# Second mixer, last 16 weight chunks: the low parts come from an accumulating transfer in place of VectorE

## The chip, the cores and the metric

The program runs on one core of a Trainium2 chip. Its engines are TensorE (PE in the profile; PEld is its weight load), VectorE (DVE), ScalarE (ACT), GpSimd (POOL) and SyncE (SP); the last two also issue the transfers of this kernel. The metric is the device time of one execution in microseconds (us), the median of several runs. Lower is better.

## The reference

Two transformer stacks follow each other on 256 tokens of width 1024, with 256 context tokens beside them in the first stack. The change lies in the first stack, whose second layer's mixer is cut to this:

```python
def _token_mixer(h, w_in, w_out, ...):
    z = h @ w_in
    u, v, q, f_fw, f_bw, i, og = jnp.split(z, cuts, axis=-1)
    a_out = _gmlp_spatial(u, v, w_s, b_s, g_v)
    o, s_f, s_b = _hgrn_bidir(q, f_fw, f_bw, i, lb_f, lb_b, s0_f, s0_b)
    o = _rmsnorm(o, g_o.reshape(HGRN_HEADS, HGRN_V)).reshape(B, L, B_W)
    b_out = o * jax.nn.silu(og)
    return jnp.concatenate([a_out, b_out], axis=-1) @ w_out, s_f, s_b
```

`_gmlp_spatial` multiplies gelu(u) by a mixed and normalised gelu(v). `_hgrn_bidir` is a gated linear scan over the tokens in both directions. All is float32; a matrix product with the weights is made here of three products of a faster type, in which each factor is split into a high and a low part.

## The kernel before, in words

Weights come from HBM in a fixed list of chunks (`plan`), mostly 128x1024 float32 (512 KB). For each chunk class `Weights` does three things. `load` (L171) issues the transfer into one of 4 buffers named `raw`, from SP. `hi_to` (L221) copies `raw` on ScalarE into `hi`, of the type that TensorE multiplies faster, which rounds it; there are 6 such buffers. `do` (L237) subtracts on VectorE, `lo` = `raw` - `hi`, into one of 5 buffers. A chunk's `raw` buffer is loaded anew once `lo` is made.

`mm3` multiplies: `hi` by the high part of the activations (L415), `hi` by their low part (L416), and `lo` by their high part (L417). A chunk of 128 columns and 256 tokens is 24 such matmuls.

The program is written in one order and every engine runs its own part of it in that order. `step` writes a chunk's matmuls, then what is to be done with the result of the chunk before (`flush`), then `ahead_hi`, which prepares later chunks, then `tick`, which advances the generators in `side`, then `ahead_lo`. `fits` says how far ahead a chunk may be prepared, by the ring of buffers.

The end of the second layer's mixer takes these chunks in this order: four of `og` (called OG0 to OG3 here), four of `u` (U0 to U3), and eight of `w_out` (WO0 to WO7). While OG and U run, the scan's second half (`hg`) advances by one level per chunk. One level is a product on TensorE (`scores`, L921), two products on VectorE (L997, L1000), a regrouping copy on ScalarE (`keys`, L928, output `Y`) that the next level's `scores` needs, and a masked copy (L1008; from the sixth level on copies on ScalarE, L1013). The spatial part (`gmlp`) runs beside it: squares on ScalarE (L1125), a power on GpSimd (L461), a scaling on ScalarE (L1132, output `vg`), and a product on TensorE (L1137).

WO0 to WO3 are then taken together: first each chunk's products with two of the eight inputs, chunk by chunk, and so on as inputs get ready, the last two of them made by L1085 from `yb`. WO4 to WO7 follow one by one. Behind WO7 come the sums of squares (L490), a broadcast (L504), and the next block's inputs (L523, L531).

Of the kernel before, what the change touches and what calls it, by code (L numbers as in the profile page):

```python
# [7 lines left out]
F32 = mybir.dt.float32  # L8
F32R = mybir.dt.float32r
U8 = mybir.dt.uint8  # L10
AF = mybir.ActivationFunctionType
ALU = mybir.AluOpType
# [97 lines left out]
class Pair:  # L110


    def __init__(self, hi, lo=None):
        self.t = [hi, lo]
# [2 lines left out]
        return self.t[i[1]][i[0], i[2]]  # L117


class Weights:  # L120


# [3 lines left out]
    def __init__(self, nc, flat, rawp, hlp, chunks, nraw, nhl):  # L126
        self.nc, self.flat, self.rawp, self.hlp = nc, flat, rawp, hlp
        self.sizes = [p[3] * p[5] for p in chunks]
        self.nraw, self.nhl = nraw, nhl
        self.offs = np.concatenate([[0], np.cumsum(np.array(self.sizes) * 128)]).tolist()  # L130
        self.units, self.ring, self.loads, self.work = [], [], [], []
        j = 0
        while j < len(chunks):
            p = chunks[j]
            u = len(self.units)
            if p[0].endswith("_w1") and (p[0][:4], p[1]) in FAST and p[4] // 128 >= FIRST_FAST:
                self.units += [(k, len(self.loads), j) for k in "axys"]
                self.work += [("s2", u), ("lo", u), ("lo", u + 1), ("s4", u), ("lo", u + 2), ("lo", u + 3)]
                self.loads.append(("p", j))
                j += 2  # L140
            else:
                self.units.append(("n", len(self.loads), j))
                self.work.append(("lo", u))
                self.loads.append(("n", j))
                j += 1
        r = 0
        for k, _, _ in self.units:
            self.ring.append(r)
            r += k != "s"
        self.n = len(self.units)  # L150
        self.n_load = self.n_hi = self.n_work = self.n_take = self.freed = 0
        self.n_pair = self.freed_pair = 0
        self.raw, self.hl, self.made, self.did = {}, {}, set(), {None}
        self.cur, self.held = 0, set()
        self.sp, self.room = None, 0
# [44 lines left out]
    def fits(self, u, part):  # L200

        if u >= self.n or self.units[u][1] >= self.n_load:
            return False
        if self.units[u][0] == "s":
            return sum(self.units[v][0] == "s" for v in self.made | self.held if v < u) < self.room
        return self.ring[u] <= self.ring[self.base] + self.nhl - 1 - (part == "lo")

    def ready(self, u):

# [3 lines left out]
    def hi_to(self, i):  # L213
        while self.n_hi <= min(i, self.n - 1):
            u = self.n_hi
            while not self.ready(u):
                self.do()
            self.dma_to(self.units[u][1])
            s = self.source(u)
            t = self.tile(u, "hi")  # L220
            self.nc.scalar.activation(out=t[:, :s.shape[-1]], in_=s, func=AF.Copy)  # L221
            self.hl[u] = Pair(t)
            self.made.add(u)
            self.n_hi += 1

    def do(self):

        k, u = self.work[self.n_work]
        _, l, j = self.units[u]
        self.dma_to(l)  # L230
        if k == "lo":
            self.hi_to(u)
            s = self.source(u)
            c = s.shape[-1]
            t = self.tile(u, "lo")
            w = self.hl[u]
            self.nc.vector.tensor_tensor(out=t[:, :c], in0=s, in1=w[:, 0, :c].bitcast(F32), op=ALU.subtract)  # L237
            w.t[1] = t
            if self.units[u][0] in "ns":
                self.raw.pop(l)  # L240
                self.freed += 1
                self.freed_pair += self.units[u][0] == "s"
        else:
            w, x = self.raw[l][:2]
            o, i = (x, w[:, 0:512]) if k == "s2" else (w, w[:, 512:1024])
            self.nc.vector.tensor_tensor(
                out=o[:, 512:1024], in0=(x[:, 0:512] if k == "s2" else x[:, 512:1024]), in1=i, op=ALU.add)
        self.did.add((k, u))
        self.n_work += 1
# [1917 lines left out]
```

## Time and profile before

| | before |
|---|---|
| median of 3 runs | 2401.54 us (2400.47 to 2401.78) |
| the profiled execution, its time | 2399.38 us |
| its span, first to last instruction | 2397.6 us |
| busy share of the span: PE, DVE, ACT, POOL | 99%, 69%, 44%, 4% |
| mean granted clock of TensorE | 0.999 |

In the rows of stretches stand the stretch and its length, then the busy time and the count of instructions of PE, PEld, DVE, ACT and POOL, the granted clock, the share of the transfer engines and GB/s. The times of the rows below count from the first instruction of the span. A busy share is a mean over stages that differ; the change lies between some 1490 us and 1580 us. The end of a matmul is modelled in this profile, so the distance between starts says more than its length.

### The profile page before, as it was taken

How to read it: one execution, taken by the hardware profiler on the slowest of the kernel's cores; microseconds unless marked ns; L12 is line 12 of the kernel's file. 1: busy time of each engine (PE TensorE's matmuls, PEld its weight loads, DVE VectorE, ACT ScalarE, POOL GpSimd, SP SyncE). 2: the span in 40 equal slices, each digit the busy share in tenths (PEclk: the TensorE clock that was granted, in tenths of full speed). 3: DMA queues.
4: the chain of work that ended last, by engine and by line, in shares of the span. 5: the costliest groups of instructions: out<-in, count | busy, mean ns of one | idle time of the engine just before them, and what ended most of it. 6: DMA issues, size and time to landing. Idle time of an engine off the chain costs nothing.

```text
span 2397.6 us, 39387 instructions
## 1 busy us (share of the span) xinstructions
PE 2368.5 (99%) x15852; PEld 2157.5 (90%) x15852; DVE 1652.1 (69%) x2670; ACT 1058.4 (44%) x1741; POOL 91.3 (4%) x136
## 2 busy tenths in 40 slices
PE   7999999999999999999999999999999999999999
PEld 5888888999888888898899999999999999999999
DVE  6788986637468888877575665765567677558653
ACT  4322223455342222244353454654466556446642
POOL 0000000000000000000101000000002000010000
PEclk9999999999999999999999999999999999999999
DMA  8555652222245556534555532355555465553663
GB/s 316 209 210 179 225 187 95 89 71 71 79 148 199 206 194 217 170 104 121 144 159 148 146 98 88 97 177 185 187 184 173 133 204 186 193 167 110 208 193 125
DMA packets 117447, 383.31 MB, mean 160 GB/s; under 512 B 12936, under 2 KB 19080, under 8 KB 117008
## 3 DMA queue, kind: packets, MB, share of 16 engines
q1 hardware_dynamic: 112368, 371.88, 46.0%
q0 software_dynamic: 4896, 8.92, 2.2%
q8 instruction: 124, 2.03, 0.3%
q14 instruction: 59, 0.48, 0.1%
HBM read 379.68 MB, written 1.06 MB: 159 GB/s over the span
## 4 chain that ended last, share of the span: by engine, by line
PE 91%; DVE 4%; issue 2%; ACT 2%; DMA 0%; POOL 0%; POOLq 0%; SPq 0%; DVEq 0%; ACTq 0%
PE mm L416 24%; PE mm L417 24%; PE mm L415 24%; PE mm L691 7%; PE mm L921 2%; PE mm L1459 2%; PE mm L1458 2%; PE mm L1460 2%; DVE lo L237 1%; PE mm L1115 1%; PE mm L1116 1%; PE mm L1117 1%; ACT hi L221 1%; PE aux L504 0%; PE mm L1555 0%
## 5 line engine op out<-in xcount | busy, mean ns | idle before, releaser
L221 ACT ACTIVATE hi<-raw 128x1024 fp32r<-128x1024 f32 (+2 forms) x544 | 554.3, 1029 | 425.0 <-PE mm L416 251.4
L415 PE MATMUL mm<-h,hi 128*128 128x256 f32 (+1 forms) x2188 | 726.2, 332 | 3.6 <-ACT h L531 2.4
L417 PE MATMUL mm<-h,lo 128*128 128x256 f32 (+1 forms) x2188 | 721.3, 330 | 0.4 <-DVE lo L237 0.2
L237 DVE TENSOR_TENSOR lo<-raw,hi 128x1024 fp32r<-128x1024 f32 (+2 forms) x544 | 642.7, 1188 | 105.2 <-PE mm L417 54.4
L416 PE MATMUL mm<-l,hi 128*128 128x256 f32 (+1 forms) x1804 | 614.3, 340 | 1.1 <-DVE l L1340 0.2
L415 PEld LDWEIGHTS mm<-h,hi 128*128 128x128 f32 x2188 | 413.1, 189 | 44.8 <-ACT h L531 2.6
L417 PEld LDWEIGHTS mm<-h,lo 128*128 128x128 f32 x2188 | 413.0, 189 | 42.9 <-DVE lo L237 1.2
L415 PE MATMUL mm<-g,hi 128*128 128x256 f32 (+1 forms) x1258 | 409.0, 325 | 0.0
L416 PE MATMUL mm<-g,hi 128*128 128x256 f32 (+1 forms) x1258 | 408.6, 325 | 0.0
L417 PE MATMUL mm<-g,lo 128*128 128x256 f32 (+1 forms) x1258 | 408.6, 325 | 0.0
L416 PEld LDWEIGHTS mm<-l,hi 128*128 128x128 f32 x1804 | 340.7, 189 | 43.9 <-DVE l L532 2.7
L399 DVE CUSTOM_DVE_ANT_0 jk<-ada,condb,vec 128x1024 f32<-128x1024 f32 x256 | 328.3, 1282 | 9.3 <-ACT condb L392 4.1
L417 PEld LDWEIGHTS mm<-g,lo 128*128 128x128 f32 x1258 | 236.6, 188 | 22.1
L415 PEld LDWEIGHTS mm<-g,hi 128*128 128x128 f32 x1258 | 236.7, 188 | 21.9
L416 PEld LDWEIGHTS mm<-g,hi 128*128 128x128 f32 x1258 | 236.7, 188 | 21.9
L538 DVE SCALAR_TENSOR_TENSOR xT<-mm,mods,xT 128x256 f32<-128x256 f32 x192 | 85.7, 479 | 119.3 <-PE mm L417 119.1
L767 ACT ACTIVATE g<-t 128x512 fp32r<-128x512 f32 (+1 forms) x71 | 40.2, 566 | 260.6 <-DVE t L765 260.6
L416 PE MATMUL mm<-h,hi 128*128 128x256 f32 x512 | 143.9, 281 | 0.0
L1458 PE MATMUL mm<-hi,h 128*128 128x256 f32 x384 | 111.1, 289 | 0.0
L1459 PE MATMUL mm<-lo,h 128*128 128x256 f32 x384 | 107.4, 280 | 0.1
L1460 PE MATMUL mm<-hi,h 128*128 128x256 f32 x384 | 107.3, 279 | 0.0
L765 DVE TENSOR_TENSOR t<-t,mm 128x512 f32<-128x512 f32 (+1 forms) x71 | 42.8, 603 | 78.6 <-PE mm L417 76.0
(329 smaller groups left out, 3294.3 us busy)
## 6 DMA issues: line engine op xcount, KB each, us to landing
raw<-wflat SPq DMA_DIRECT2D x463, 512.0 KB, 3.4
ada<-adaT SPq DMA_DIRECT2D x128, 512.0 KB, 4.2
raw<-wflat SPq DMA_DIRECT2D x64, 448.0 KB, 3.4
wy<-wflat SPq DMA_DIRECT2D x34, 256.0 KB, 4.5
ada<-ada SPq DMA_DIRECT2D x16, 512.0 KB, 10.0
wx<-wflat SPq DMA_DIRECT2D x17, 256.0 KB, 3.0
wx<-wflat POOLq DMA_DIRECT2D x17, 256.0 KB, 5.2
wy<-wflat POOLq DMA_DIRECT2D x17, 256.0 KB, 5.5
```

The lines of the kernel that those rows point to most:

```text
L221: self.nc.scalar.activation(out=t[:, :s.shape[-1]], in_=s, func=AF.Copy)
L237: self.nc.vector.tensor_tensor(out=t[:, :c], in0=s, in1=w[:, 0, :c].bitcast(F32), op=ALU.subtract)
L399: nc.vector.tensor_tensor_reduce(out=jk, in0=t, in1=condb[:, c, :], scale=1.0, scalar=V(f"bada{l}")[:, j:j + 1], op0=ALU.mult, op1=ALU.add ...
L415: nc.tensor.matmul(out, whi, xhi, start=start, stop=False)
L416: nc.tensor.matmul(out, whi, xlo, start=False, stop=False)
L417: nc.tensor.matmul(out, wlo, xhi, start=False, stop=stop)
L538: nc.vector.scalar_tensor_tensor(out=xT[:, o, t0:t1], in0=ps[:, t0:t1], scalar=gate(l, i, o, 0 if t0 == 0 else 1), in1=xT[:, o, t0:t1], op ...
L691: nc.tensor.matmul(ps[:, :256], a, b, start=start and k + m == 0, stop=k == 3 and m == 2, skip_group_check=not start)
L921: nc.tensor.matmul(sl(p, i), sl(Y, b + i), x(b + i), start=True, stop=True)
L1458: nc.tensor.matmul(p[:, :256], xhi, whi, start=(k == 0), stop=False)
L1459: nc.tensor.matmul(p[:, :256], xhi, wlo, start=False, stop=False)
L1460: nc.tensor.matmul(p[:, :256], xlo, whi, start=False, stop=(k == 7))
```

## The change

For 16 chunks (OG0 to OG3, U0 to U3 and WO0 to WO7 of the second layer) `lo` is no longer made by VectorE. `hi_to` makes both parts: ScalarE copies `raw` into `hi` as before, then writes the negated `hi` into `lo`, and GpSimd issues a transfer from `raw` to `lo` that adds, on the way, to what stands there. `do` then only frees the `raw` buffer in the count; the next load into that buffer waits for the adding transfer. Since `lo` must have a buffer at the time of `hi`, these chunks may be prepared 4 ahead and no longer 5.

```diff
+def lo_by_dma(p):
+
+    return p[1] == 1 and (p[0] == "w_out" or p[0] == "w_in" and p[4] in range(0, 512) or p[0] == "w_in" and p[4] >= 3072)
...
+        self.by_dma = {u for u, (k, _, j) in enumerate(self.units) if k == "n" and lo_by_dma(chunks[j])}
...
-        return self.ring[u] <= self.ring[self.base] + self.nhl - 1 - (part == "lo")
+        return self.ring[u] <= self.ring[self.base] + self.nhl - 1 - (part == "lo" or u in self.by_dma)
...
             t = self.tile(u, "hi")
             self.nc.scalar.activation(out=t[:, :s.shape[-1]], in_=s, func=AF.Copy)
             self.hl[u] = Pair(t)
+            if u in self.by_dma:
+                c = s.shape[-1]
+                lo = self.tile(u, "lo")
+                self.nc.scalar.activation(out=lo[:, :c], in_=t[:, :c].bitcast(F32), func=AF.Copy, scale=-1.0)
+                self.nc.gpsimd.dma_start(out=lo[:, :c].bitcast(F32), in_=s, accum_op=ALU.add)
+                self.hl[u].t[1] = lo
...
-            t = self.tile(u, "lo")
             w = self.hl[u]
-            self.nc.vector.tensor_tensor(out=t[:, :c], in0=s, in1=w[:, 0, :c].bitcast(F32), op=ALU.subtract)
-            w.t[1] = t
+            if u not in self.by_dma:
+                t = self.tile(u, "lo")
+                self.nc.vector.tensor_tensor(out=t[:, :c], in0=s, in1=w[:, 0, :c].bitcast(F32), op=ALU.subtract)
+                w.t[1] = t
```

The order of TensorE and of SP stays as it was, and VectorE's is the same without the 16 subtractions. ScalarE's changes at three places that the prediction speaks of. Rows of the changed kernel carry its own line numbers: L227 is the copy into `hi`, L232 the negation, L233 the adding transfer, and from L250 on each number is 13 above that of before (L941 there is L928 here).

The first place is ScalarE from the last product of `v` on. Before, from the two copies that start at 1500.29 us:

```order
L221 ACTIVATE hi<-raw 128x1024 x2
L936 COPY at<-mm 128x512
L928 COPY Y<-Wt_13112 128x512
L1125 ACTIVATE t,ss<-vg 128x128 x4
L1196 ACTIVATE vg<-mm 128x256
L1132 ACTIVATE vg<-vg,ss 128x128 x4
L1196 ACTIVATE vg<-mm 128x256
L221 ACTIVATE hi<-raw 128x1024 x2
L1125 ACTIVATE t,ss<-vg 128x128 x4
L1099 ACT_TABLE_LOAD
L1099 ACTIVATE yb<-mm 128x256
L221 ACTIVATE hi<-raw 128x1024
```

Of the change, the same stretch as far as the second pair:

```order
L227 ACTIVATE hi<-raw 128x1024
L232 ACTIVATE lo<-hi 128x1024
L227 ACTIVATE hi<-raw 128x1024
L232 ACTIVATE lo<-hi 128x1024
L949 COPY at<-mm 128x512
L941 COPY Y<-Wt_13113 128x512
L1138 ACTIVATE t,ss<-vg 128x128 x4
L1209 ACTIVATE vg<-mm 128x256
L1145 ACTIVATE vg<-vg,ss 128x128 x4
L1209 ACTIVATE vg<-mm 128x256
L227 ACTIVATE hi<-raw 128x1024
L232 ACTIVATE lo<-hi 128x1024
```

Each copy has its negation behind it, ahead of the work that stood there; the copies are those of a chunk one place earlier in the list than before.

The second place is ScalarE at the scan's last level, behind U2's result. Before, where the last row is the copy of WO4:

```order
L1085 ACTIVATE YE<-a_12357 128x256
L221 ACTIVATE hi<-raw 128x1024
L928 COPY Y<-Wt_13112 128x512
L1013 COPY at<-mm 32x4x32 x4
L1103 ACTIVATE t<-mm 128x256
L221 ACTIVATE hi<-raw 128x1024
```

Of the change, where the last two rows are the copy and the negation of WO3:

```order
L1098 ACTIVATE YE<-a_12357 128x256
L227 ACTIVATE hi<-raw 128x1024
L232 ACTIVATE lo<-hi 128x1024
L941 COPY Y<-Wt_13113 128x512
L1026 COPY at<-mm 32x4x32 x4
L1116 ACTIVATE t<-mm 128x256
L227 ACTIVATE hi<-raw 128x1024
L232 ACTIVATE lo<-hi 128x1024
```

WO3's high part has moved from ahead of the last `Y` to behind it, with the negation after it.

The third place is ScalarE behind the last two inputs of `w_out`. Before, where the copies are those of WO5 and WO6:

```order
L1085 ACTIVATE h_13800<-yb 128x256
L1085 ACTIVATE h_13804<-yb 128x256
L221 ACTIVATE hi<-raw 128x1024
L543 ACT_TABLE_LOAD
L543 ACTIVATE dummy<-epsc 128x1
L475 ACTIVATE acc<-xT 128x256
L221 ACTIVATE hi<-raw 128x1024
```

Of the change, where they are those of WO4 and WO5:

```order
L1098 ACTIVATE h_13810<-yb 128x256
L1098 ACTIVATE h_13814<-yb 128x256
L227 ACTIVATE hi<-raw 128x1024
L232 ACTIVATE lo<-hi 128x1024
L556 ACT_TABLE_LOAD
L556 ACTIVATE dummy<-epsc 128x1
L488 ACTIVATE acc<-xT 128x256
L227 ACTIVATE hi<-raw 128x1024
L232 ACTIVATE lo<-hi 128x1024
```

Here too each chunk is one place later than before, and has a negation more.

## Rows read from the trace of the kernel before

**Rows 1.** The page's span, and VectorE's subtraction from 1500 to 1560 us

```profile
span 2397.6 us, 39387 instructions
L237 DVE TENSOR_TENSOR lo<-raw,hi 128x1024 fp32r<-128x1024 f32 x12 | 14.5, 1217 | 1.6 <-ACT hi L221 1.6
```

**Rows 2.** Busy time by stretch; the last row sums 1500 to 1560 us

```profile
1520.00:1530.00 10.00, 9.78 (x82) 9.38 (x81) 8.96 (x17) 5.45 (x10) 0.00 (x0) 1.00 0.40 135
1530.00:1540.00 10.00, 9.17 (x77) 8.76 (x76) 8.77 (x16) 7.07 (x15) 0.00 (x0) 1.00 0.33 107
...
sum 60.00, PE 57.86 PEld 56.57 DVE 45.98 ACT 37.40 POOL 5.99; mean PE 9.64 PEld 9.43 DVE 7.66 ACT 6.23 POOL 1.00
```

**Rows 3.** ScalarE in order of time, OG chunks: start, length, instruction, [idle before]

```profile
1500.29 2.01 ACT L221 ACTIVATE hi<-raw 128x1024 fp32r<-128x1024 f32 x2
1502.31 0.59 ACT L936 COPY at<-mm 128x512 f32<-128x512 f32 x1
...
1514.70 0.68 ACT L928 COPY Y<-Wt 128x512 f32<-128x512 f32 x1
```

**Rows 4.** TensorE in order of time, the scan's level behind OG2

```profile
1515.93 1.13 PE L921 MATMUL mm<-Ut,Y 128*128 128x128 f32 x8
```

**Rows 5.** ScalarE in order of time, the scan's last level

```profile
1537.74 0.62 ACT L928 COPY Y<-Wt 128x512 f32<-128x512 f32 x1 [0.22 <-DVE Wt L997]
1538.27 1.06 ACT L1013 COPY at<-mm 32x128 f32<-32x128 f32 x4
1539.35 0.39 ACT L1103 ACTIVATE t<-mm 128x256 f32<-128x256 f32 x1
1539.63 1.05 ACT L221 ACTIVATE hi<-raw 128x1024 fp32r<-128x1024 f32 x1
```

**Rows 6.** TensorE in order of time, WO3's first product with its low part

```profile
1541.63 0.28 PE L416 MATMUL mm<-YE,hi 128*128 128x256 f32 x1
1542.79 0.39 PE L417 MATMUL mm<-YE,lo 128*128 128x256 f32 x1 [0.88 <-DVE lo L237]
```

**Rows 7.** Transfers by queue: count, KB, median us to landing; last, from 1160 to 1176 us

```profile
raw<-wflat SPq DMA_DIRECT2D x463, 512.0 KB, 3.4
...
wx<-wflat POOLq DMA_DIRECT2D x17, 256.0 KB, 5.2
wy<-wflat POOLq DMA_DIRECT2D x17, 256.0 KB, 5.5
...
wx<-wflat POOLq DMA_DIRECT2D x1, 256.0 KB, 4.0
```

**Rows 8.** The page's queues: packets, MB, share of 16 engines' span

```profile
q1 hardware_dynamic: 112368, 371.88, 46.0%
q0 software_dynamic: 4896, 8.92, 2.2%
```

**Rows 9.** ScalarE in order of time, behind the last two inputs of w_out

```profile
1557.00 1.05 ACT L221 ACTIVATE hi<-raw 128x1024 fp32r<-128x1024 f32 x1
...
1559.78 1.05 ACT L221 ACTIVATE hi<-raw 128x1024 fp32r<-128x1024 f32 x1
```

**Rows 10.** TensorE in order of time, WO4's first products

```profile
1560.40 0.28 PE L416 MATMUL mm<-YE,hi 128*128 128x256 f32 x1
1560.51 0.28 PE L417 MATMUL mm<-YE,lo 128*128 128x256 f32 x1
```

**Rows 11.** Busy time by stretch behind the mixer; the clock is the third number from the end

```profile
1576.00:1578.00 2.00, 0.00 (x0) 0.00 (x0) 1.82 (x3) 0.54 (x2) 0.00 (x0) 0.50 0.42 139
1578.00:1580.00 2.00, 1.98 (x8) 1.74 (x9) 1.99 (x6) 1.18 (x3) 0.00 (x0) 0.50 0.87 299
1580.00:1582.00 2.00, 2.00 (x11) 2.00 (x11) 2.00 (x7) 1.24 (x3) 0.00 (x0) 0.50 0.21 86
1582.00:1584.00 2.00, 2.00 (x16) 2.00 (x16) 1.70 (x5) 1.65 (x3) 0.00 (x0) 0.80 0.00 0
```

## The prediction

> **What bounds the kernel now.** I read the page first. TensorE is busy for 99% of a span of 2397.6 us [rows 1], so a gain can only come from stretches in which it stands idle. I then looked at the stretches around the change. From 1500 to 1560 us TensorE is busy 57.86 of 60 us, VectorE 45.98 and ScalarE 37.40 [rows 2]. The 2.14 us in which TensorE is idle are all that this stretch can give back, which is 0.09% of the span. VectorE looks full between 1520 and 1540 us (8.96 and 8.77 of 10), and the one wait for a low part in the stretch is 0.88 us, at WO3 [rows 6]. So the subtractions are near the path there, but they do not hold up much. In order of time ScalarE then shows how it shares its work between weight copies and the scan [rows 3, 5], and the rows of transfers show what an adding transfer takes [rows 7]. The idle time behind the mixer, up to 1578 us [rows 11], is a norm that the change does not touch.
>
> **The change, part by part.** It takes 16 subtractions of 1.2 us from VectorE [rows 1]. I count the gain of that at the idle time that it could remove, which is inside the terms below. It adds 16 negations on ScalarE. The nearest row is the copy of the same size: two of them run from 1500.29 to 1502.31 us, so 1.0 us each [rows 3]. It adds 16 adding transfers of 512 KB from GpSimd, whose queue else holds only a few small norms here.
>
> How long such a transfer takes no row shows. The adding transfers of another phase, of 256 KB and with HBM as their source, land 5.2 us after issue in the median, and 4.0 us where few others run [rows 7]. There are 34 of them, and they fill 2.2% of 16 engines' span [rows 8]: 0.022 x 2397.6 / 34 = 1.55 us of all engines each. Twice the bytes would add another 1.55 us, so I take 5.2 + 1.55 = 6.8 us. The lower end is 4.0 us, as if bytes cost nothing and the queue were free. The upper end is 10.4 us, twice the median.
>
> The plain load of 512 KB lands in 3.4 us [rows 7]. The Trainium skill's page "DMA: Bandwidth & Descriptors" (section "Anatomy of one DMA — SWDGE (gpsimd) path") fits a transfer from GpSimd with about 2.0 us plus its bytes over 436 GB/s, an estimate of 3.2 us here. The trace disagrees for transfers that add: 4.0 to 5.5 us at half the size. By that estimate the sum below would be some 9 us in place of 20.
>
> *First term, ScalarE in the OG chunks.* Six negations stand ahead of the `Y` that starts at 1514.70 us: OG0's ahead of the sigmoids, then those of OG1, OG2, OG3, U0 and U1. The copies ahead of it stay six. `Y` thus starts 6.0 us later, for ScalarE has nothing in these rows to give way [rows 3]. It ended at 1515.38, and the product that needs it began at 1515.93 us [rows 4], a cover of 0.55 us. TensorE is late by 5.45 us there. Before that, the scaled `vg` is late by three negations, and TensorE waits for it too; that is a part of the same 5.45. In the levels of U it can win back what it idled between 1520 and 1540 us, 0.22 + 0.83 = 1.05 us [rows 2], since VectorE is now lighter. Term: 4.4 us.
>
> *Second term, WO3.* It is copied after the last `Y` and no longer before. Before, from that `Y` (1537.74) to the copy that stands in the new one's place (1539.63) ScalarE took 1.89 us [rows 5]. With copy and negation `lo` can be sent at 1541.63 on the same clock, and lands at 1548.4. TensorE could have gone on at 1542.79 - 0.88 = 1541.91 [rows 6]. It waits 6.5 us, of which 0.88 were there before. Term: 5.6 us (2.8 at 4.0 us, 9.2 at 10.4 us). Nothing lies behind this in TensorE's queue that could go first: the products of WO0 to WO2 precede it and the scan's end follows.
>
> *Third term, WO4.* Its copy now stands where WO5's was, at 1557.00 [rows 9]. With the negation it is sent at 1559.0 and lands at 1565.8; its product starts at 1560.51 [rows 10]. Term: 5.3 us (2.5 and 8.9). WO5's copy came 2.78 us after the one before it [rows 9], now 3.78: it begins at 1560.8, is sent at 1562.8 and lands at 1569.6. TensorE needs it 24 products of 0.12 us after WO4's, at 1568.6, so 1.0 us more; the next term covers that.
>
> *Fourth term, the clock.* After TensorE stood idle from 1576 to 1578 us its granted clock reads 0.50 (1.2 GHz) until 1582 and 0.80 until 1584 [rows 11]. From 1578 on that costs 4 x 0.5 + 2 x 0.2 = 2.4 us. I count it behind both long waits: 4.8 us, which takes in WO5's 1.0.
>
> The SP queue holds the next `raw` load until the adding transfer has read the old one, some 7 us later than before, and behind it on SP stand only further weight loads. Four buffers make a round of 2.0 + 6.8 + 3.4 us for four chunks, 3.05 us a chunk; the chunks of this stretch take TensorE 2.8 us and a level on top. I cost this at nothing; without the levels it would cost 0.25 us a chunk. GpSimd's power for `gmlp` stands behind two transfers in its queue, but both are ready before the squares that it needs, so it costs nothing either.
>
> Sum: 4.4 + 5.6 + 5.3 + 4.8 = 20.1 us. The profiled execution took 2399.4 us (its span is 2397.6), which gives 2419.5; the median of the runs is 2401.5, so I predict 2421 us for the median. At 4.0 us with one fall of the clock the sum is 4.4 + 2.8 + 2.5 + 2.4 = 12.1, at 10.4 us it is 4.4 + 9.2 + 8.9 + 4.8 = 27.3.
>
> **The rivals.** *Not slower.* ScalarE is idle for 60 - 37.40 = 22.6 us in the stretch [rows 2], more than 16 negations. If it takes them in its gaps and the low parts land in time, TensorE gets back up to 2.1 us: 2399.4 us. Against it: the gaps lie behind 1520 us and the first negations ahead of it, and a transfer for WO4 would have to land in 1560.51 - 1559.0 = 1.5 us, from which point on this rival decides; none of the rows of transfers is that short.
>
> *Transfers as quick as plain loads.* Source and target both lie on the chip, which may be cheaper than the rows with HBM. At 3.4 us the second term is 2.2, the third 1.9, WO5 waits 1.0 and the clock holds: 4.4 + 2.2 + 1.9 + 1.0 = 9.5 us, 2411 us. The page of the Trainium skill named above would have it so.
>
> *Transfers in each other's way.* The plain queue moves 371.88 MB in 46.0% of the span [rows 8], 1.55 us for 512 KB; an adding one needs 3.1. A chunk asks for 4.65 us of the engines, and from WO4 on TensorE takes a chunk each 2.8 us. WO6 and WO7 would be late as well. The upper end of 10.4 us stands for this: 27.3 us, 2429 us. For it: the rows of 5.2 us against 4.0 where few run.
>
> **How the numbers follow.** The forecast has 0.51, not slower 0.09, quick transfers 0.20, transfers in each other's way 0.20. The forecast's own range is 12.1 to 27.3 us, 2414 to 2429. The range of 8 in 10 takes in the quick rival at 2411 with some room, 2408, and most of the slow one, 2432; outside are the rival that is not slower and a part of the slow one. A measurement of this kernel can tell about 0.2% (4.8 us) from no change. Only the first rival lies within it or below: same 0.07 and faster 0.02 of its 0.09. I add 0.01 to each for an overestimate of the first term, which leaves slower 0.89.
>
> **What would show it.** First term: ScalarE's `Y` of the second level some 6 us later against OG0's first product, and TensorE waiting for ScalarE at L1137's or L921's place. Second and third: waits of L417's place for a transfer into `lo`, at WO3 and WO4, of 5 to 7 us. The rows of transfers should give `lo<-raw` near 6.8 us. Fourth: a clock of 0.50 behind those waits. The prediction is wrong if these transfers land within 2 us, if ScalarE's negation is far shorter than 1.0 us, or if TensorE's waits in the stretch stay near 2 us in all.

## The result, and the profile after

| | before | after |
|---|---|---|
| median of 4 runs each | 2401.01 us (2400.08 to 2401.78) | 2422.97 us (2422.20 to 2425.45) |
| the profiled execution: its time, its span | 2399.38 us, 2397.6 us | 2422.71 us, 2420.9 us |
| mean granted clock | 0.999 | 0.994 |

The change makes the kernel slower by a ratio of 1.0094 (95% interval 1.0082 to 1.0105), 22.0 us. The prediction was 2421.0 us, with a range of 2408 to 2432.

I read the waits first. TensorE in order of time, after, those rows that show idle time ahead of them (start, length, instruction, [idle before <- releaser]):

```profile
1511.07 2.23 PE L1150 MATMUL mm<-wsT,vg 128*128 128x128 f32 x8 [3.03 <-ACT vg L1145]
1522.18 1.23 PE L934 MATMUL mm<-Ut,Y 128*128 128x128 f32 x8 [1.08 <-ACT Y L941]
...
1546.54 0.38 PE L430 MATMUL mm<-YE,lo 128*128 128x256 f32 x1 [0.93 <-DMA lo<-raw]
1548.99 0.49 PE L430 MATMUL mm<-YE,lo 128*128 128x256 f32 x1 [1.48 <-DMA lo<-raw]
1553.98 0.58 PE L430 MATMUL mm<-YE,lo 128*128 128x256 f32 x1 [3.44 <-DMA lo<-raw]
1577.58 0.58 PE L430 MATMUL mm<-YE,lo 128*128 128x256 f32 x1 [3.23 <-DMA lo<-raw]
1583.29 0.39 PE L430 MATMUL mm<-YE,lo 128*128 128x256 f32 x1 [0.22 <-DMA lo<-raw]
1589.66 0.38 PE L430 MATMUL mm<-YE,lo 128*128 128x256 f32 x1 [0.45 <-DMA lo<-raw]
1594.24 0.35 PE L503 MATMUL aux<-ones,acc 128*128 128x1 f32 x2 [1.73 <-DVE acc L492]
```

The first two are the spatial part's product and the second level's, which wait for ScalarE; the second answers to [rows 4]. The next six are the first low-part products of WO1 to WO5 and WO7; that of WO3 answers to [rows 6], that of WO4 to [rows 10]. The one wait of before for a low part, 0.88 us, has become six, 9.75 us in all.

ScalarE in order of time, after, at the places of [rows 3], [rows 5] and [rows 9]:

```profile
1521.47 0.65 ACT L941 COPY Y<-Wt 128x512 f32<-128x512 f32 x1
...
1542.86 0.60 ACT L941 COPY Y<-Wt 128x512 f32<-128x512 f32 x1
...
1544.72 1.05 ACT L227 ACTIVATE hi<-raw 128x1024 fp32r<-128x1024 f32 x1
1545.80 1.06 ACT L232 ACTIVATE lo<-hi 128x1024 fp32r<-128x1024 f32 x1
...
1570.68 1.05 ACT L227 ACTIVATE hi<-raw 128x1024 fp32r<-128x1024 f32 x1
1571.76 1.06 ACT L232 ACTIVATE lo<-hi 128x1024 fp32r<-128x1024 f32 x1
...
1589.94 1.06 ACT L227 ACTIVATE hi<-raw 128x1024 fp32r<-128x1024 f32 x1 [5.43 <-DMA raw<-wflat]
```

The `Y` that started at 1514.70 us now starts 6.8 us later. WO3 is copied behind the last `Y`. The last row is new: a copy of the next block's first weights waits 5.43 us for its load. The transfers themselves, after, by tile (nanoseconds min/median/max, then from issue to landing in us), by GpSimd in order of time (WO3's and WO4's issue), and by kind and queue as in [rows 7, 8]:

```profile
L232 ACT ACTIVATE lo<-hi x16: 1056/1060/1063, 1494.5 to 1580.3; 128x1024 fp32r<-128x1024 f32 x16
L233 POOL DMA_DIRECT2D lo<-raw x16: 850/859/919, 1495.9 to 1581.7; - x16
...
DMA to landing us min/median/max: 4.4/5.7/8.0
```

```profile
1547.15 0.85 POOL L233 DMA_DIRECT2D lo<-raw  x1 [3.06 <-ACT lo L232]
1573.12 0.90 POOL L233 DMA_DIRECT2D lo<-raw  x1 [4.02 <-ACT lo L232]
```

```profile
lo<-raw POOLq DMA_DIRECT2D x16, 512.0 KB, 5.7
...
q0 software_dynamic: 7200, 17.30, 4.0%
```

WO3's transfer is issued at 1547.15 and its product starts at 1553.98, 6.8 us later. For WO4 that distance is 4.5 us. The difference lies in what else is under way. Busy time in these two stretches, each from the issue to the landing, then by stretches of 10 us, after (columns as in [rows 2, 11]):

```profile
1547.15:1553.94 6.79, 1.91 (x10) 1.42 (x8) 0.43 (x1) 0.73 (x2) 0.85 (x1) 0.64 0.96 260
1573.12:1577.54 4.42, 1.23 (x11) 1.03 (x9) 1.12 (x4) 4.38 (x7) 1.46 (x2) 0.87 0.60 119
...
1540.00:1550.00 10.00, 7.59 (x59) 7.19 (x59) 4.46 (x10) 7.26 (x14) 2.06 (x3) 0.96 0.94 227
1550.00:1560.00 10.00, 6.56 (x34) 6.27 (x34) 1.14 (x4) 0.63 (x2) 0.00 (x0) 0.53 0.50 144
...
1570.00:1580.00 10.00, 6.77 (x48) 6.57 (x48) 3.85 (x9) 9.78 (x14) 2.45 (x3) 0.82 0.44 86
1580.00:1590.00 10.00, 9.33 (x65) 8.83 (x65) 1.96 (x3) 2.76 (x5) 1.03 (x2) 0.84 1.05 263
```

While WO3's transfer is under way the engines that move data are full (0.96), and they move 260 GB/s, over three times its own bytes. While WO4's is under way they move 119 GB/s, which in 4.42 us is its own 512 KB and nothing else. Behind WO3's wait the granted clock reads 0.53. The queue q0 took 4.0% x 2420.9 - 2.2% x 2397.6 = 44 us more of 16 engines for 16 transfers, 2.75 us each, where a plain load of the same size takes 1.55 us by the prediction's reckoning of [rows 8].

To see where the time went I lined up the same instruction in every run. The table gives the starts in before's profiled execution, and below it each run's offset to them in us. "Entry" is the stage's first product (an offset there is older than the change). OG behind OG2 is OG3's first product, then come the first product of `w_out`, the first behind the four first parts of WO0 to WO3, the first that needs the scan's end, WO4's first low part, the norm's sums and the next block's first product.

```
            entry     OG3     WO0  4 parts scan end     WO4   norm  next block    span
before    1492.82 1517.70 1539.33  1543.37  1545.96 1560.51 1572.75    1578.03 2397.60
after       +0.12   +6.35   +5.09   +11.63   +13.71  +17.07  +21.49     +21.56  +23.30
e1_lead     +0.98   +1.97   +2.06    +2.06    +2.07   +2.07   +4.88      +5.57   +6.00
e2_negate   +0.67   +6.70   +7.27    +7.56    +7.57   +7.51  +14.51     +15.40  +16.60
e3_og_u     +0.86   +7.08  +10.71   +10.55   +10.55  +10.59  +10.59     +10.58  +13.60
e4_w_out    +0.80   +0.80   +1.96    +8.26    +9.37  +12.74  +17.13     +17.55  +23.20
e5_lead5    +1.03   +7.23   +5.98    +7.78    +9.42   +9.40  +14.23     +14.28  +16.10
e6_filler   +0.12   +6.32   +5.08   +10.91   +10.91  +14.28  +20.07     +20.85  +21.70
e7_half     -0.31   +5.91   +4.65    +3.74    +3.85   +6.11  +10.33     +10.39  +11.70
e8_three    +1.21   +1.21   +1.27    +0.87    +0.88   +0.92   +0.92      +0.92   +1.40
e9_raw2     +0.61   +6.83   +5.59    +7.44    +8.68   +8.68  +12.20     +12.27  +14.00
e10_pool    +1.22   +8.96   +7.63   +16.73   +19.12  +24.39  +29.95     +30.02  +30.30
e11_og_raw4 +1.01   +7.22   +5.74    +5.76    +5.77   +5.80   +5.79      +5.79   +8.10
```

Read along the row "after": 6.2 us are lost by OG3 (5.0 of them left at WO0), 6.5 in the four first parts, 2.1 up to the scan's end, 3.4 at WO4, 4.4 from there to the norm, and 1.8 behind it.

### The profile page after: what moved, and what is told of

It is laid out like the page before. It is cut to its first block, busy times and chain, and to the rows that moved or that the text cites. A ratio compares the mean times of both kernels' runs of the same rounds, so it can differ in the third digit from the quotient of the medians.

```text
span 2420.9 us, 39423 instructions
## 1 busy us (share of the span) xinstructions
PE 2377.8 (98%) x15852; PEld 2165.3 (89%) x15852; DVE 1635.1 (68%) x2654; ACT 1074.0 (44%) x1757; POOL 102.9 (4%) x152
## 3 DMA queue, kind: packets, MB, share of 16 engines
HBM read 379.68 MB, written 1.06 MB: 157 GB/s over the span
## 4 chain that ended last, share of the span: by engine, by line
PE 89%; ACT 3%; issue 3%; DVE 3%; DMA 2%; POOL 0%; POOLq 0%; SPq 0%; DVEq 0%; ACTq 0%
PE mm L429 23%; PE mm L430 23%; PE mm L428 23%; PE mm L704 7%; PE mm L934 2%; PE mm L1472 1%; PE mm L1473 1%; PE mm L1471 1%; ACT hi L227 1%; DMA raw<-wflat 1%; PE mm L1128 1%; PE mm L1129 1%; PE mm L1130 1%; DVE lo L250 1%; DMA lo<-raw 1%
## 5 line engine op out<-in xcount | busy, mean ns | idle before, releaser
L227 ACT ACTIVATE hi<-raw 128x1024 fp32r<-128x1024 f32 (+2 forms) x544 | 554.3, 1028 | 432.5 <-PE mm L429 251.2
L250 DVE TENSOR_TENSOR lo<-raw,hi 128x1024 fp32r<-128x1024 f32 (+2 forms) x528 | 623.1, 1187 | 112.7 <-PE mm L430 53.8
```

## Experiments

My theory had three causes: ScalarE's negations, the length of the adding transfer together with copies put one place later, and the clock behind the waits. Each run below takes one of them alone or away. The time beside a run is that of before on the same chip; where two runs are compared, each is first set against its own.

**The lead alone (e1_lead).** Before, with the 16 chunks prepared 4 ahead and no longer 5; nothing else.

```diff
-        return self.ring[u] <= self.ring[self.base] + self.nhl - 1 - (part == "lo")
+        return self.ring[u] <= self.ring[self.base] + self.nhl - 1 - (part == "lo" or u in self.by_dma)
```

> The kernel before, with one thing of the change: the 16 chunks may be copied to their high part only 4 ahead, not 5. VectorE still subtracts, nothing is negated or sent. Theory (the time goes to negations on ScalarE, then to low parts that land late, then to the clock): VectorE's subtractions keep their place and still end in time, so the time stays within 1 us of before, 2400 to 2402 us. Rival (the shorter lead by itself is the cost, since the copies of WO3 and WO4 move behind the scan's last Y and the last inputs): slower by 8 us or more, 2409 us and up.

Measured 2406.18 us beside 2401.10, ratio 1.0021 (1.0011 to 1.0030), 5.1 us. Both expectations missed it. The table puts 1.0 us behind OG2 and 2.8 us at the norm. TensorE's waits from 1480 to 1640 us (us in total, times, longest) show the second:

```profile
PE aux L496 <- DVE acc L485: 3.8, 1, 3.8
...
PE mm L927 <- ACT vg L1138: 0.7, 1, 0.7
```

With one chunk less in hand, copy, subtraction, the update of the activations and their square wait for each other in turn in WO4 to WO7: ScalarE's copies lie 3.1 us apart there (1562.13, 1565.25, 1568.36), where before they lay 1.9 apart and ran ahead. The norm's sum waits 3.8 us where it waited 1.0. The lead is not free, even where no transfer runs.

**The negation without the transfer (e2_negate).** The change, shorter lead included, without its transfers: ScalarE negates, then VectorE subtracts into the same `lo`.

```diff
-                self.nc.gpsimd.dma_start(out=lo[:, :c].bitcast(F32), in_=s, accum_op=ALU.add)
...
+            t = w.t[1] if u in self.by_dma else self.tile(u, "lo")
+            self.nc.vector.tensor_tensor(out=t[:, :c], in0=s, in1=w[:, 0, :c].bitcast(F32), op=ALU.subtract)
```

> As the run with the shorter lead, and ScalarE also writes the 16 negations into the low part's buffer, where VectorE's subtraction then writes over them. No adding transfer. It prices the work on ScalarE alone. Theory: TensorE is late by 5 to 6 us at the level behind OG2, as in the change, wins back nothing in U because VectorE keeps its subtractions, and waits little at WO3 and WO4: 6 to 8 us above before, 2407 to 2409 us. Rival (ScalarE has room for the negations, the transfers alone cost time): within 2 us of before.

Measured 2416.15 us, ratio 1.0065 (1.0050 to 1.0080), 15.1 us, which both expectations missed. TensorE's waits in the same window, then ScalarE between two chunks of `w_out`:

```profile
PE mm L428 <- DVE lo L248: 4.4, 4, 1.2
PE aux L501 <- DVE acc L490: 4.0, 1, 4.0
PE mm L932 <- ACT Y L939: 3.0, 4, 1.2
PE mm L1148 <- ACT vg L1143: 2.8, 1, 2.8
```

```profile
1572.48 0.42 ACT L489 ACTIVATE t<-xT 128x256 f32<-128x256 f32 x1 [1.69 <-DVE xT L549]
```

By OG3 this run is 6.7 - 0.7 = 6.0 us late, after 6.2. So the first term needs no transfer. The lead alone cost 1.0 of these 6.0 us, but the run with the lead back (e5_lead5, below) is late by 6.2 us at the same place, so the first term needs no shorter lead either: what these runs share are the negations on ScalarE. In the levels of U this run wins nothing back (6.0 us at OG3, 6.6 at WO0), where the change wins 1.3; here VectorE keeps its subtractions. The surprise is the 7.0 us between WO4 and the norm. There each chunk's copy, negation, subtraction, update and square follow each other, 4.15 us a chunk, and WO5 to WO7 wait about 1.05 us each. ScalarE is not full there: it idles 1.69 us of each round until the update is made. It is the chain that has grown by a negation.

**Half the chunks (e3_og_u, e4_w_out).** The first run changes only OG and U, the second only `w_out`.

```diff
+    return p[1] == 1 and (p[0] == "w_in" and p[4] in range(0, 512) or p[0] == "w_in" and p[4] >= 3072)
```

```diff
+    return p[1] == 1 and p[0] == "w_out"
```

> The change for the eight chunks OG0 to U3 alone; the eight of w_out are subtracted by VectorE with the lead of before. Theory: the first term without the others. 5 to 6 us late behind OG2, some of it won back in U, no wait for a transfer: 4 to 6 us above before, 2405 to 2407 us. Rival (the transfers get into each other's way from the start, and every chunk waits): half of the change's loss or more, 2412 us and up.

> The change for the eight chunks of w_out alone; OG and U are subtracted by VectorE with the lead of before. Theory: the second to fourth terms without the first. Nothing is lost behind OG2; WO3 waits about 6 us and WO4 3 to 5 us for their transfers, and the clock falls behind each: 14 to 18 us above before, 2415 to 2419 us; with the run for OG and U it adds up to the change's 22 us within 3. Rival (the transfers of w_out are late only because ScalarE is late already, or because the ones of U are still in the queue): 6 us or less, 2407 us and below.

OG and U: 2408.81 us, ratio 1.0034 (1.0021 to 1.0047). `w_out`: 2420.75 us, ratio 1.0084 (1.0069 to 1.0099). Both lie above what I had expected, by 1.8 us each. The `w_out` part is the dearer one. In its profile TensorE waits five times for transfers, 11.3 us. Together they cost 27.4 us where the whole change costs 22.0, so they do not add up within the 3 us that I had named. The profiled execution of OG and U, which at 2412.98 us is 4 us above its median, lost 3.6 us at 1536 us, which the whole change does not lose. ScalarE in order of time there, at the last levels:

```profile
1538.01 1.06 ACT L227 ACTIVATE hi<-raw 128x1024 fp32r<-128x1024 f32 x1 [4.80 <-DMA raw<-wflat]
1538.97 0.57 ACT L991 COPY wt<-mm 128x512 f32<-128x512 f32 x1
1539.43 0.62 ACT L941 COPY Y<-Wt 128x512 f32<-128x512 f32 x1
```

A copy into `hi` waits 4.8 us for its load, and the level's `Y` stands behind it. The prediction had costed exactly this, a load held back by an adding transfer, at nothing. The next run tests it.

**More raw buffers for OG and U (e11_og_raw4).** The run of OG and U with four more buffers for raw weights, used by every second of its chunks.

```diff
+            t = self.rawx.tile([128, 1024], F32, tag="rawx", name="raw", bufs=4)
```

> The OG and U chunks alone by negation and adding transfer (the lead 4 for these), with four more buffers for raw weights, used by every second of these chunks. Theory (the 3.6 us wait of TensorE for a level's copy at 1536 us in the run of OG and U alone comes from ScalarE waiting 4.8 us for a raw load that could not start while an adding transfer still read its buffer): that wait is gone, the first w_out product comes at +5 to +7 us instead of +10.7, time 2405 to 2407.5 where that run had a median of 2408.8. Rival (the load is late because the DMA engines are shared): ScalarE still waits 3 us or more for raw weights there, 2408 to 2411.

Measured 2406.59 us, ratio 1.0027 (1.0017 to 1.0037), as the theory had it. ScalarE's wait for raw weights is gone from the profile, and WO0 starts at +5.7 us in place of +10.7. The medians, each against its own runs of before, differ by 1.8 us only (7.71 and 5.95), and the run without these buffers was profiled in its slowest execution; how long the wait was in the others was not recorded. Buffers alone took it away, with the same transfers under way, so the held buffer is the likelier cause; that the runs without them spread over 5.8 us (2407.19 to 2412.98) keeps this from being settled.

**The lead back (e5_lead5).** The change, with the low parts of every second of its chunks in three buffers of their own, so that 5 chunks may be prepared ahead again.

```diff
-        return self.ring[u] <= self.ring[self.base] + self.nhl - 1 - (part == "lo" or u in self.by_dma)
+        if part == "lo" and u in self.by_dma and u % 2 == 0:
+            return self.lox.tile([128, 1024], F32R, tag="lox", name="lo", bufs=3)
...
+        return self.ring[u] <= self.ring[self.base] + self.nhl - 1 - (part == "lo")
```

> The change whole, but the low parts of every second of its 16 chunks go into a ring of three buffers of their own, so that copies may run 5 chunks ahead again as before the change (in the change 4). Theory (the w_out waits come from two things, a copy put one place later by the shorter lead and the transfer's own 5.7 us): with the lead back WO3's transfer is issued ahead of the last doubled level and WO4's ahead of the state product, so the waits for a low part of WO2, WO3 and WO4 (1.5, 3.4 and 3.2 us in the change) shrink to under 1 us each and the clock behind them does not fall; ScalarE's 6 us behind the OG chunks stay. 2409 to 2413 us. Rival (the transfer's time is what decides, the lead matters little): the three waits stay over 2 us each and the time at 2419 or more.

Measured 2415.63 us beside 2400.46, ratio 1.0061 (1.0045 to 1.0076): 15.2 us above before where the change was 22.0, so 6.8 us come back, between the two expectations. TensorE in order of time:

```profile
1550.58 0.39 PE L432 MATMUL mm<-YE,lo 128*128 128x256 f32 x1 [2.67 <-DMA lo<-raw]
1573.33 0.39 PE L432 MATMUL mm<-YE,lo 128*128 128x256 f32 x1 [0.45 <-DMA lo<-raw]
1578.97 0.58 PE L432 MATMUL mm<-YE,lo 128*128 128x256 f32 x1 [2.55 <-DMA lo<-raw]
```

The waits of WO1, WO2 and WO4 are gone, WO3's is 2.67 instead of 3.44, and WO6 now waits 2.55 (counted by products; the expectation of the next run calls it WO7). WO3's transfer is issued 3 us earlier (1544.13), but TensorE, no longer held by WO1 and WO2, comes earlier too. So both things count, and the lead is about a third of the loss.

**Lead and raw buffers (e9_raw2).** The same lead with two buffers for it, and two more raw buffers, each used by every third chunk.

> The change with its lead of 5 (low parts of every third of the 16 chunks in a ring of two of their own) and two more buffers for raw weights, used by every third of these chunks. Theory (a raw buffer is held until the adding transfer that reads it has landed, so the loads behind it start late, ScalarE's copies wait for them, and the last w_out chunks with it): ScalarE's waits for raw weights at 1480 to 1640 us (6.2 us in the run with lead 5) fall under 2 us, the wait for the low part of WO7 (2.55 us there) under 1.2 us, time 1.5 to 3 us under that run, 2412.5 to 2414. Rival (the DMA engines are full at 1520 to 1550 us, busy share 0.96 to 1.04, and loads that start earlier only take longer): the same waits within a third, 2415 to 2417.

Measured 2414.09 us beside 2400.64, ratio 1.0055 (1.0040 to 1.0070). ScalarE's waits for raw weights in this window fall from 6.2 us to 1.1, as the theory had it, but TensorE's waits hardly move:

```profile
1549.87 0.50 PE L446 MATMUL mm<-YE,lo 128*128 128x256 f32 x1 [2.36 <-DMA lo<-raw]
1572.57 0.38 PE L446 MATMUL mm<-YE,lo 128*128 128x256 f32 x1 [0.40 <-DMA lo<-raw]
1578.27 0.39 PE L446 MATMUL mm<-YE,lo 128*128 128x256 f32 x1 [2.61 <-DMA lo<-raw]
```

Against before it is 13.5 us in place of 15.2, a difference about as large as two such runs differ by. The late load was not what made WO6 late (2.61 us of wait here, 2.55 there); its product comes 6.3 us after its transfer's issue (1571.97).

**Half the bytes (e7_half).** Each transfer carries the left 512 of 1024 columns.

```diff
-                self.nc.gpsimd.dma_start(out=lo[:, :c].bitcast(F32), in_=s, accum_op=ALU.add)
+                self.nc.gpsimd.dma_start(out=lo[:, :c // 2].bitcast(F32), in_=s[:, :c // 2], accum_op=ALU.add)
```

> The change whole, but each adding transfer carries only the left half of the columns (256 KB); the right half of each low part keeps the negated high part, so the low parts of these 16 chunks are wrong there. Theory (the transfer takes some 3.2 us and 2.5 us per 512 KB): median from issue to landing 3.9 to 4.8 us, the waits for WO3 and WO4 1 to 1.5 us shorter each, time 2419 to 2421. Rival (a cost for each transfer that does not hang on its size decides): median 5.2 us or more and the same waits within 0.4 us, 2422.5 or more.

Measured 2412.61 us beside 2400.46, ratio 1.0052 (1.0039 to 1.0066): 12.2 us above before where the change was 22.0. That is 9.8 us less, far more than I expected. The transfers by tile, and TensorE's waits in the window:

```profile
DMA to landing us min/median/max: 3.2/3.3/7.3
```

```profile
PE mm L1150 <- ACT vg L1145: 3.0, 1, 3.0
PE mm L430 <- DMA lo<-raw: 2.5, 2, 2.1
```

The median falls from 5.7 to 3.3 us, all waits in the four first parts vanish, and with them the fall of the clock (it reads 1.00 from 1540 to 1570 us). The first term stays as it was (5.91 + 0.31 = 6.2 us at OG3), as it must if the negations make it. So the size of the transfer decides the waits here. It is not all of a transfer's time: with nothing beside it a transfer takes 4.4 us in the change and 3.2 here, 1.2 us less for 256 KB less, so by an estimate from these two some 2.0 us are left that do not hang on the size. The medians differ by 2.4 us; the further 1.2 us go with less company, since WO3's transfer lands here 3.2 us after its issue in place of 6.8.

**The clock (e6_filler).** The change, with products into a tile that nobody reads ahead of WO2 (10), WO3 (24) and WO4 (22), in TensorE's waiting time.

```diff
+            def fill(w, n):
+                p = aux_ps()
+                for _ in range(n):
+                    nc.tensor.matmul(p[:, :256], w[:, 0, 0:128], Y[early[0]][:, 0, :256], start=True, stop=True)
```

> The change whole, and 10, 24 and 22 products of 256 columns whose result nobody reads on TensorE ahead of the first products of WO2, WO3 and WO4 (about 1.2, 2.8 and 2.6 us), inside the time in which it waits for their low parts. Theory (part of the loss is the clock, which falls to about half behind a TensorE that has waited): the granted clock of 1550 to 1560 us stays above 0.8 (in the change 0.53) and 3 to 5 us come back, 2418 to 2420. Rival (the clock's fall there has another cause, or costs nothing of its own): the granted clock of that stretch stays under 0.65 and the time within 1 us of the change's or above it.

Measured 2423.39 us, ratio 1.0094 (1.0080 to 1.0107): nothing comes back. Yet the clock did what the theory said. Busy time by stretch, then TensorE in order of time (WO4 and WO5):

```profile
1550.00:1560.00 10.00, 10.00 (x85) 9.84 (x86) 1.38 (x5) 1.49 (x3) 0.00 (x0) 1.00 0.51 150
...
1570.00:1580.00 10.00, 7.22 (x60) 6.81 (x58) 2.16 (x5) 8.76 (x13) 3.48 (x4) 1.00 0.73 160
1580.00:1590.00 10.00, 7.61 (x62) 7.41 (x63) 2.35 (x4) 2.56 (x4) 0.00 (x0) 1.00 0.99 272
```

```profile
1574.79 0.39 PE L430 MATMUL mm<-YE,lo 128*128 128x256 f32 x1 [0.66 <-DMA lo<-raw]
1580.51 0.38 PE L430 MATMUL mm<-YE,lo 128*128 128x256 f32 x1 [2.63 <-DMA lo<-raw]
```

The clock stays at 1.00 (2.4 GHz) where it had fallen to 0.53, and at the scan's end the run stands at +10.9 in place of +13.7 us. The fall behind WO3 thus cost about 2 us: from the four first parts to the scan's end the change loses 2.1 us and this run nothing. But behind WO4 TensorE, now at full clock, comes to the last chunks sooner than their low parts: one wait there is 2.63 us where the change has 0.22. From WO4's first low-part product to WO5's it is 1583.29 - 1577.58 = 5.71 us in the change and 1580.51 - 1574.79 = 5.72 here, at either clock, since WO5's transfer sets it. At the norm 1.4 us of the 2.8 are left in this execution, which is 2.2 us under the run's median, and in the medians nothing. Where a transfer that lands later decides, a slower TensorE only hides the wait for it; the two do not add.

**The negation on GpSimd (e10_pool).**

```diff
-                self.nc.scalar.activation(out=lo[:, :c], in_=t[:, :c].bitcast(F32), func=AF.Copy, scale=-1.0)
+                self.nc.gpsimd.tensor_scalar(out=lo[:, :c], in0=t[:, :c].bitcast(F32), scalar1=-1.0, scalar2=None, op0=ALU.mult)
```

> The change whole, but the 16 negations of the high part on GpSimd, just ahead of the transfers that it issues, in place of ScalarE. Theory (the 6.2 us behind the OG chunks are ScalarE's own time in negations, which lie ahead of the second level's copies): the first product behind the third OG chunk is at most 2 us late instead of 6.2, the waits for the low parts in w_out stay or grow by what a negation takes longer there, time 2416 to 2420. Rival (GpSimd's negation is slow enough, 4 us or more, or it disturbs VectorE, so that the low parts of OG and U come late themselves): TensorE waits for low parts in OG and U, and the time is 2424 or more.

Measured 2429.75 us, ratio 1.0119 (1.0104 to 1.0134), the time of the rival, but not by its road: no product of OG or U waits for a low part. GpSimd's part by tile, and what ScalarE waits for from 1480 to 1640 us:

```profile
L232 POOL TENSOR_SCALAR lo<-hi x16: 2787/3116/3247, 1495.7 to 1589.1; 128x1024 fp32r<-128x1024 f32 x16
```

```profile
ACT hi L227 <- DMA raw<-wflat: 16.3, 5, 6.4
...
ACT vg L1145 <- POOL ss L474: 9.9, 2, 6.1
```

The negation takes 3.1 us here against 1.06 on ScalarE, and `gmlp`'s power stands behind two of them in GpSimd's queue, so that `vg` is late by another road and OG3 by 7.7 us. This run therefore says nothing for or against ScalarE as the cause of the first term; e2_negate and e5_lead5 do.

**Three chunks (e8_three).** Only U3, WO0 and WO1 by transfer, with the lead of 5.

```diff
+    return p[1] == 1 and (p[0] == "w_out" and p[4] < 256 or p[0] == "w_in" and p[4] == 384)
```

> Only three of the 16 chunks (the last of U and the first two of w_out) by negation and adding transfer, their low parts in a ring of three buffers of their own, so the lead stays 5; the other 13 as before the change. Theory (in this stretch VectorE is what the levels wait for, ScalarE has room, and these three low parts are wanted 15 us or more after their copy): no wait for a transfer at TensorE, three subtractions of 1.0 us gone from VectorE, 0 to 2 us faster than before, 2399 to 2401. Rival (each negation on ScalarE delays a level's copy by its 1.06 us as in the OG chunks): 1 to 3 us slower, 2402 to 2404.

Measured 2401.11 us beside 2400.46, ratio 1.0002 (0.9993 to 1.0011): no change. TensorE's waits from 1480 to 1640 us:

```profile
PE mm L936 <- ACT Y L943: 1.6, 2, 1.2
...
PE mm L432 <- DVE lo L252: 0.5, 1, 0.5
```

No product waits for a transfer. Three subtractions are gone from VectorE, the wait at WO3 is 0.5 in place of 0.88, and the waits for `Y` are 1.6 us. For these three chunks, whose transfers have time enough, the change brings nothing; their subtractions held up next to nothing. No run here beats the kernel before.

## Why the prediction came out right

The terms by the norm add up to 21.4 us, forecast 20.1. The paths were mostly those of the prediction; that the sum came so near is in part luck, for the third term was 1.9 us too long and the fourth 1.7 too short.

**What bounds it** held in the main: the stretch had 2.14 us of idle time to win, and the run of three chunks won nothing measurable. But the norm behind the mixer, which the change was not to touch, was touched: its sum waits 1.73 us in place of 1.0, and 3.8 in the run with the shorter lead alone.

**First term** (4.4 us): measured 5.0 at WO0 and 6.2 at OG3. `Y` was to start 6.0 us later and did so by 6.8, 0.12 of it older, and 1.3 us were won back in U where 1.05 were forecast. e2_negate and e5_lead5 together show the cause.

**Second term** (5.6 us): measured 6.5. WO3's transfer went out 4.3 us behind the last `Y`'s start, by the prediction 3.9, and its product came 6.8 us later, the very figure taken. That figure was an estimate from rows of another phase; it is right where the engines are full and wrong elsewhere, so its fit here is luck. The sign that was named, waits of 5 to 7 us at WO3 and WO4, did not show: they are 3.44 and 3.23 us. At WO3 that is because WO1 and WO2, for which no wait was counted, already wait 0.93 and 1.48 us for their own transfers; WO3's landing ends the last of the three waits, so the sum is right all the same.

**Third term** (5.3 us): measured 3.4. Here the same 6.8 us was the step that failed. WO4's transfer ran with nothing beside it and its product came 4.5 us after the issue; the issue was 0.4 us later than forecast.

**Fourth term** (4.8 us): behind WO3 2.1 us are lost by the scan's end, and the filler shows that this is the clock. From WO4 to the norm it is 4.4 us: 0.22 and 0.45 us of waits at WO5 and WO7, 0.73 us more at the norm's sum (1.73 for 1.0), and 3.0 us of the rest, in which the clock reads low (0.50 from 1577 to 1583 us). That makes 6.5 us against 4.8. As a cause the term is half right: behind WO4 the filler kept the clock up and the time did not fall, since at WO5 and WO7 the transfers were next.

**Costed at nothing.** The shorter lead costs 5 us by itself in the kernel before, and 6.8 us in the change, of which the prediction held the places (WO3 and WO4 copied one later) but not the price. The held raw buffer shows after as SP's waits by the queue's own row,

```profile
SPq L177 <- DMA lo<-raw: 89.5, 16, 23.2
```

and as ScalarE's 5.43 us above, which cost nothing (+21.49 at the norm, +21.56 at the next block). In the profiled execution of OG and U alone such a wait went with 5 us at WO0; in the whole change with the lead back, buffers for it bought at most 1.7 us. So counting it as nothing did little harm in the whole change, but the reason given, that a round of buffers is short enough, is not borne out: the loads did come late, and TensorE waited for the transfers meanwhile.

**The rivals.** "Quick transfers" and "in each other's way" both have a part: 4.5 us alone, 6.8 us in a crowd, up to 8.0. The Trainium skill's page "DMA: Bandwidth & Descriptors" (section "Anatomy of one DMA — SWDGE (gpsimd) path") gives an estimate of 3.2 us for this transfer; the shortest of 16 took 4.4 us, so the trace disagrees for transfers that add.

**Open.** The sum of the terms by the norm is 21.4 us and the profiled span is 23.2 us longer, entry taken off. The last 1.8 us come far behind the mixer; 1.1 us of them lie near 1800 to 1830 us, and 0.9 us between 1865 and 2160 us also shows in the run with no transfer at all. What makes them was not tried. Why OG and U and `w_out` cost 27.4 us apart and 22.0 together is shown in part. As far as the norm they do add: 4.8 us for OG and U with more raw buffers and 16.3 for `w_out`, entry taken off, make 21.1 where the change loses 21.4. The excess lies elsewhere: OG and U lose some 2 us more without these buffers, and the profiled execution of `w_out`, the slowest of its four, loses 4.0 us at one place far behind the mixer, between 1810 and 1820 us on before's clock, where the change loses 1.1. There a copy waits long for its load:

```profile
1830.52 1.06 ACT L227 ACTIVATE hi<-raw 128x1024 fp32r<-128x1024 f32 x1 [8.64 <-DMA raw<-wflat]
```

Why that load is so late in this execution is not shown.

## What to carry to other kernels

Work taken from an engine that hardly anything waits for, and replaced by a longer path through two others, is paid for at each place where the result is wanted soon; price it from the issue to the first use, per chunk, with what else the transfer engines do at that moment. Count how long each buffer is held (here a source is held until the transfer that reads it has landed) and what a lead shorter by one costs with all else equal. And do not add the price of a slower clock to that of a wait for a later transfer: the one hid the other here, and taking the first away alone brought nothing.

## What the runs showed of the hardware

- An adding transfer of 512 KB within the chip took 4.4, 5.7 and 8.0 us (min, median, max) from issue to landing, one of 256 KB 3.2, 3.3 and 7.3 us; a plain load of 512 KB 3.4 us in the median. It took about 2.75 us of all 16 engines, 1.8 times a plain load; where it ran alone they were busy for 0.60 of its 4.42 us, 2.65 us.
- Each issue of it kept GpSimd busy for 0.86 us.
- The same negation of 128x1024 took 1.06 us on ScalarE and 3.1 us on GpSimd.
- With products whose results nobody reads in TensorE's waiting time, the granted clock stayed at 1.00 (1550 to 1560 us) where it had read 0.53.
